# An MLP in four parts on one Trainium2 core: the second product of a part mixed with the first product of the next

## The chip, the cores and the metric

The kernel runs on one core of a Trainium2 chip. The metric is the device time of one execution in microseconds. The kernel before takes 1968.92 us (median of 3 runs, 1968.87 to 1968.93).

The core's engines work beside each other and meet through semaphores: TensorE (PE in the profile; PEld is its weight load) multiplies into PSUM, which has eight banks of 128 x 512 float32; VectorE (DVE) and ScalarE (ACT) work element by element and are the ones that empty PSUM here; GpSimd (POOL) works on SBUF; SyncE (SP) issues most of the loads.

## What is computed

A trunk of two layers over 256 tokens of width 2048, all in float32. Layer 0 mixes tokens by a convolution module, layer 1 by multi-head latent attention, and each is followed by the same kind of MLP, which holds the change:

```python
D_MODEL = 2048; SEQ = 256; DEPTH = 2; D_FF = 4 * D_MODEL

def sq_relu_mlp(h, w1, w2):
    return jnp.square(jax.nn.relu(h @ w1)) @ w2

for layer in range(DEPTH):
    h = rms_norm(x, norm_mixer_g[layer])
    x = x + mixer(h)            # convolution module or latent attention
    h = rms_norm(x, norm_mlp_g[layer])
    x = x + sq_relu_mlp(h, mlp_w1[layer], mlp_w2[layer])
return rms_norm(x, final_norm_g)
```

`w1` is 2048 x 8192 and `w2` 8192 x 2048, so a layer's MLP reads 128 MB of weights.

## The kernel before

**Three matmuls for one product.** Each float32 operand is split into a part `hi`, rounded to TensorE's float32r format by a copy on ScalarE (`split_into`, L412), and a part `lo = x - hi` on VectorE (L413). A product is hi·hi + lo·hi + hi·lo, three matmuls (`mm3`, L186 to L188). Weights come from HBM in raw units of 1 MB (`load`, L150, three buffers) and are split in chunks; six `hi` and six `lo` buffers (`WB = 6`) hold chunks that are ready.

**First product** (`up_unit`, L473). A group is 512 columns of `w1`. For each of 16 steps k along D and each of the group's four 128-column blocks there are two matmuls into the block's own bank: L488 multiplies `hi` of the weights by the activations' `hi` and `lo` side by side (512 columns: 256 tokens twice), and L489 `lo` of the weights by the activations' `hi` (256 columns). A group so fills four banks. `up_steps` then makes `g = relu(u)^2`: ScalarE copies one half of each bank out (L504), VectorE adds the other half (L506), then squares (L509 or L520), and the result is split as well. The RMS norm's factor is applied after the second product, as `r2` in L545.

**Second product** (`down_units`, L530). Two blocks of the hidden width make a *pair*. One pass covers two of the four 512-column blocks of the output, so with two token tiles a pair is a 2 x 2 by 2 x 2 block product. A *plain* pair (`plain_unit`) takes eight `mm3`, 24 matmuls. A pair in *Strassen's form* (`seven_unit`, in Winograd's variant) takes seven, 21 matmuls, into seven banks; for it GpSimd makes three sums of the activations (L513 to L517) when the pair's first product is done, and VectorE makes sums of the weights: L649 (two at once) and L662 (two) for each pair and pass, and these sums are split too. When a pass has done its last Strassen pair, `early` (L560) combines four of the seven banks (ScalarE copies L566 and L567, VectorE L568 and L569, GpSimd L574 and L575, VectorE L545); the other four results (three banks and one more, `Q0`) go on through the plain pairs, and `end` (L583) adds them to the residual `xs`.

**Order.** The hidden width is cut in `HALVES = 2`. Each half does its whole first product (8 groups) and then its second product in two passes (`n2`) over 16 pairs. `SEVENS` names which pairs of a half take Strassen's form: 7 of 16 in each half, in turn with plain ones. In the last pass of layer 1 the last three pairs are kept back and done by token tile, so that the final norm of one tile runs beside the other's matmuls (`finale`).

**Streaming.** `stream` (L415) runs over all units' chunks under a hand-written order (`manual_schedule`): before TensorE's work of a chunk it issues the split of the chunk five further on, and before each split one step of `todo` (the squares, the parts, `early`'s later steps). When a unit's last split is issued, the unit three further on is loaded. Each engine works its instructions off in this order.

Of the kernel before, what the change touches and what calls it, by code (L numbers as in the profile page):

```python
# [10 lines left out]
F32 = mybir.dt.float32  # L11
# [7 lines left out]
P = 128  # L19
# [7 lines left out]
W = 31  # L27
# [8 lines left out]
HALVES = 2  # L36
# [41 lines left out]
def trunk_kernel(  # L78
# [66 lines left out]
    def load(srcs, nj):  # L145

        raw = wpool.tile([P, nj, sum(src.shape[-1] for src in srcs)], F32, tag="raw", name=nm("raw"), bufs=3)
# [237 lines left out]
    NPAIR = FF // P // HALVES // 2  # L385
    N_SEVEN = len(SEVENS[0])
# [17 lines left out]
    class Chunk:  # L404
        def __init__(self, prep, run, after=(), now=None, flush=False):
            self.prep, self.run, self.after, self.now, self.flush = prep, run, after, now, flush
# [8 lines left out]
    def stream(units, todo):  # L415

        raws, parts, late = {}, {}, []

        def start(u):
            if u < len(units):  # L420
                raws[u] = load([units[u].src], units[u].nj)

        chunks = [(u, c) for u, unit in enumerate(units) for c in range(len(unit.chunks))]
        done = [0]

        def prep():
            n = done[0]
            if n == len(chunks):
                return
            done[0] += 1  # L430
            u, c = chunks[n]
            held = late[:]
            late.clear()
            if units[u].chunks[c].flush:
                while held:
                    held.pop(0)()
            more = units[u].chunks[c].prep(raws[u], parts.setdefault(u, {}))
# [4 lines left out]
            if c == units[u].last_read:  # L442
                start(u + 3)

        for u in range(3):
            start(u)
        for n, (u, c) in enumerate(chunks):
            while done[0] < min(n + WB, len(chunks)):
                prep()
                if todo:  # L450
                    todo.pop(0)()
            if done[0] == len(chunks):
                while late:
                    late.pop(0)()
                for fn in todo[: 2 if n < len(chunks) - 1 else None]:
                    todo.remove(fn)
                    fn()
            chunk = units[u].chunks[c]
            chunk.run(parts[u])
            if chunk.now is not None:  # L460
                chunk.now()
            todo += chunk.after
        while todo:
            todo.pop(0)()

    def mlp(layer, ssq, next_gain, finish=None, before=None, last_w1=None):

        w1, w2 = mlp_w1[layer], mlp_w2[layer]
        units, nkh = [], FF // P // HALVES
        r2 = small.tile([P, T], F32, tag="r2", name=nm("r2"))  # L470
        made_stage, pre = [], []

        def up_unit(hs, c0, u, ps, after):  # L473

            def chunk(h):
                def prep(raw, parts):
                    parts[h] = hi_lo(2)
                    split_into(parts[h], raw[:, 2 * h : 2 * h + 2, :])

                def run(parts):  # L480
                    if not ps:
                        ps.extend(acc_tile() for _ in range(4))
                    wh, wl = parts.pop(h)
                    for j in range(2):
                        k = 4 * u + 2 * h + j
                        for b in range(4):
                            bs = slice(b * P, (b + 1) * P)
                            nc.tensor.matmul(ps[b], wh[:, j, bs], xhl(k), start=k == 0, stop=False)  # L488
                            nc.tensor.matmul(ps[b][:, :S], wl[:, j, bs], xh(k), start=False, stop=k == KC - 1)  # L489

                return Chunk(prep, run, after if h == 1 else [])

            unit = Unit(rows(w1, 4 * u, 4, c0, NB), 4, [chunk(h) for h in range(2)])
            unit.last_read = 1
            return unit

        def up_steps(mp, hs, sevens, p, ps, b2):

            held = {}

            def square():
                v = mp.tile([P, 2, S], F32, tag="v", name=nm("v"), bufs=2)
                for b in range(2):
                    nc.scalar.activation(v[:, b, :], ps[2 * b2 + b][:, S:], AF.Copy)  # L504
                for b in range(2):
                    nc.vector.tensor_tensor(v[:, b, :], ps[2 * b2 + b][:, :S], v[:, b, :], op=ALU.add)  # L506
                if p in sevens:
                    f = mp.tile([P, 8, P], F32, tag="W", name=nm("W"), bufs=1)
                    nc.vector.scalar_tensor_tensor(  # L509
                        out=f[:, 0:4, :].rearrange("p (b t) n -> p b (t n)", b=2), in0=v, scalar=0.0, in1=v,  # L510
                        op0=ALU.max, op1=ALU.mult,
                    )
                    nc.gpsimd.tensor_tensor(  # L513
                        f[:, 4:6, :], f[:, 0:1, :].broadcast_to([P, 2, P]), f[:, 1:3, :], op=ALU.subtract
                    )
                    nc.gpsimd.tensor_tensor(f[:, 6, :], f[:, 1, :], f[:, 5, :], op=ALU.subtract)
                    nc.gpsimd.tensor_tensor(f[:, 7, :], f[:, 3, :], f[:, 6, :], op=ALU.subtract)  # L517
                    held["src"], shape, tag, n = f[:, 1:8, :], [P, 7, P], "s", N_SEVEN
                else:
                    nc.vector.scalar_tensor_tensor(out=v, in0=v, scalar=0.0, in1=v, op0=ALU.max, op1=ALU.mult)  # L520
                    held["src"], shape, tag, n = v, [P, 2, S], "g", NPAIR - N_SEVEN
# [6 lines left out]
            return square, part  # L528

        def down_units(mp, hs, sevens, hf, n2):  # L530

            last_seven = max(sevens)
            last = hf == HALVES - 1
# [21 lines left out]
            def plain(p, k, part, n, t):  # L555
                gh, gl = (a[:, k, t * P : (t + 1) * P] for a in hs[p])
                bs = n - na
                mm(outs[t, n], gh, gl, part[0][:, bs, :], part[1][:, bs, :], p == NPAIR - 1 and k == 1)

            def early():  # L560
                s1, s5 = (mp.tile([P, NB], F32, tag="v", name=nm("v"), bufs=2) for _ in range(2))
# [19 lines left out]
                return [first, second, third]  # L581
# [23 lines left out]
            def plain_unit(p):  # L605

                def chunk(k):
# [4 lines left out]
                    def run(parts):  # L612
                        if tail and p > last_seven:
                            if k == 0:
                                kept.append((p, parts))
                            if p == NPAIR - 1 and k == 1:
# [9 lines left out]
                    if k == 1 and p == NPAIR - 1 and not tail:  # L626
# [5 lines left out]
            def seven_unit(p):  # L632
# [31 lines left out]
                def t24(raw, parts):  # L664
# [4 lines left out]
                    Chunk(one, run([("P1", A11, "one", 0)]), flush=True),  # L669
# [14 lines left out]
            for p in range(NPAIR):  # L684
                chunks, last_read = seven_unit(p) if p in sevens else plain_unit(p)
                unit = Unit(rows(w2, hf * nkh + 2 * p, 2, na * NB, 2 * NB), 2, chunks)
# [4 lines left out]
        with ExitStack() as cx:  # L691
            mp = cx.enter_context(tc.tile_pool(name=f"mp{layer}", bufs=1, reuse_waits="tile"))
            todo = []
# [5 lines left out]
            for hf in range(HALVES):  # L699
                hs, sevens = {}, SEVENS[2 * layer + hf]  # L700
                for g in range(nkh // 4):
                    ps = []
                    for u in range(KC // 4):
                        after = []
                        if u == KC // 4 - 1:
                            (sa, pa), (sb, pb) = (up_steps(mp, hs, sevens, 2 * g + b2, ps, b2) for b2 in range(2))
                            after = [sa, sb, pa, pb]
                            if g == nkh // 4 - 1 and hf == 0:
                                after.append(norm)
                            if g == nkh // 4 - 1 and hf == HALVES - 1 and last_w1 is not None:  # L710
                                after.append(last_w1)
                        units.append(up_unit(hs, (hf * nkh + 4 * g) * P, u, ps, after))
                for n2 in range(NNB // 2):
                    units += down_units(mp, hs, sevens, hf, n2)

            with tc.manual_schedule():
                stream(units, todo)
# [985 lines left out]
```

## Time and profile before

| | |
|---|---|
| median of 3 runs | 1968.92 us |
| the profiled execution | 1969.05 us, its span 1966.9 us |
| TensorE busy | 1939.8 us (99%), 10892 matmuls |
| VectorE busy | 1521.8 us (77%) |
| ScalarE busy | 1070.4 us (54%) |
| GpSimd busy | 334.8 us (17%) |
| read from HBM | 363.68 MB, 186 GB/s with what is written, over the span |
| layer 0's MLP begins | 318.6 us (first L488) |
| layer 1's MLP | 1270.2 us to the end |

The span is the time from the first to the last instruction; the execution's own time is 2.15 us more. Busy times of TensorE count overlapping matmuls once, so they say nothing on how dense the matmuls are; for that one divides a stretch by the number of matmuls in it. The columns of a group of instructions are: line, engine, operation, tile written <- tiles read, shapes, count | busy us, mean ns of one | idle time of the engine just before them, and what ended it. In a timeline a row is the start, the duration, the engine, the line and the instruction.

### The profile page before, as it was taken

What the parts mean: (1) busy time and instruction counts of PE and PEld (TensorE: products, weight loads), DVE (VectorE), ACT (ScalarE), POOL (GpSimd) and SP (SyncE); (2) the same over time, 40 slices, a digit from 0 to 9 for tenths busy, and PEclk for the clock granted to TensorE, in tenths of its full rate; (3) what the DMA queues carried; (4) which work ended last, traced back from release to release, by engine and by line L of the source; (5) the groups of instructions that cost most, each with busy time, mean ns of one, the idle gap of its engine ahead of it and who ended that gap; (6) DMA issues with size and microseconds to landing.
All of it is one profiled execution on the core that took longest, in us unless ns stands there. A gap on an engine that the chain in (4) does not pass through costs nothing.

```text
span 1966.9 us, 28422 instructions
## 1 busy us (share of the span) xinstructions
PE 1939.8 (99%) x10892; PEld 1695.0 (86%) x10892; DVE 1521.8 (77%) x2123; ACT 1070.4 (54%) x1511; POOL 334.8 (17%) x284
## 2 busy tenths in 40 slices
PE   7999999999999999999999999999999999999998
PEld 7999888888888888888899998888888888888886
DVE  5999866666899777689886665566689986668897
ACT  5556655454555545455576665544456554455555
POOL 5999300111000011100001410011100001110000
PEclk9999999999999999999999999999999999999999
DMA  8666455656566765656656445566657676665663
GB/s 237 178 186 179 142 188 185 187 179 191 176 208 201 227 188 183 192 187 195 213 167 182 118 147 180 184 186 191 188 164 229 193 222 190 193 193 189 219 191 130
DMA packets 210503, 367.61 MB, mean 187 GB/s; under 512 B 15416, under 2 KB 89792, under 8 KB 210112
## 3 DMA queue, kind: packets, MB, share of 16 engines
q1 hardware_dynamic: 209344, 363.63, 59.6%
q10 hardware_dynamic: 1024, 2.17, 0.3%
q8 instruction: 85, 1.39, 0.3%
q14 instruction: 50, 0.41, 0.1%
HBM read 363.68 MB, written 2.10 MB: 186 GB/s over the span
## 4 chain that ended last, share of the span: by engine, by line
PE 94%; DVE 2%; ACT 1%; DMA 1%; issue 1%; POOL 0%; POOLq 0%; DVEq 0%; ACTq 0%; SPq 0%
PE acc L488 24%; PE acc L186 15%; PE acc L187 15%; PE acc L188 15%; PE acc L489 12%; PE acc L775 3%; PE acc L774 3%; PE acc L773 3%; PE acc L242 1%; PE sum L823 0%; DVE lo L413 0%; PE acc L1471 0%; DMA xs<-in_x 0%; DMA raw<-in_mlp_w 0%; PE acc L1335 0%
## 5 line engine op out<-in xcount | busy, mean ns | idle before, releaser
L413 DVE TENSOR_TENSOR lo<-raw,hi 128x1024 fp32r<-128x1024 f32 (+1 forms) x512 | 610.6, 1203 | 282.0 <-ACT hi L412 279.6
L412 ACT ACTIVATE hi<-raw 128x1024 fp32r<-128x1024 f32 (+1 forms) x512 | 512.9, 1012 | 480.4 <-PE acc L488 317.4
L488 PE MATMUL acc<-xt,hi 128*128 128x512 f32 x2048 | 713.8, 393 | 0.0
L489 PE MATMUL acc<-xt,lo 128*128 128x256 f32 x2048 | 574.4, 280 | 0.0
L488 PEld LDWEIGHTS acc<-xt,hi 128*128 128x128 f32 x2048 | 384.4, 188 | 88.1
L489 PEld LDWEIGHTS acc<-xt,lo 128*128 128x128 f32 x2048 | 385.3, 188 | 0.1
L186 PE MATMUL acc<-hi,gh 128*128 128x512 f32 x576 | 224.3, 389 | 0.0
L188 PE MATMUL acc<-lo,gh 128*128 128x512 f32 x576 | 224.1, 389 | 0.0
L187 PE MATMUL acc<-hi,gl 128*128 128x512 f32 x576 | 224.1, 389 | 0.0
L412 ACT ACTIVATE hi<-T 128x1024 fp32r<-128x1024 f32 x112 | 119.1, 1064 | 159.8 <-DVE T L662 103.6
L186 PE MATMUL acc<-hi,sh 128*128 128x512 f32 x520 | 203.5, 391 | 1.5 <-DVE v L506 1.5
L160 ACT ACTIVATE hi<-raw 128x1024 fp32r<-128x1024 f32 (+2 forms) x184 | 179.9, 1005 | 42.2 <-PE acc L187 38.2
L188 PE MATMUL acc<-lo,sh 128*128 128x512 f32 x520 | 202.8, 390 | 0.0
L161 DVE TENSOR_TENSOR lo<-raw,hi 128x1024 fp32r<-128x1024 f32 (+2 forms) x118 | 133.2, 1147 | 65.1 <-ACT hi L160 59.5
L875 DVE SCALAR_TENSOR_TENSOR sum<-ub,w_dw,sum 128x256 f32<-128x256 f32 x400 | 162.7, 478 | 7.6 <-ACT sum L831 6.5
L161 POOL TENSOR_TENSOR lo<-raw,hi 128x1024 fp32r<-128x1024 f32 x66 | 157.5, 2410 | 24.2 <-ACT hi L160 24.2
L513 POOL TENSOR_TENSOR W<-W 128x256 f32<-128x256 f32 x28 | 21.8, 779 | 800.3 <-ACT hi L412 622.1
L187 PE MATMUL acc<-hi,sl 128*128 128x512 f32 x392 | 152.5, 389 | 0.0
L413 DVE TENSOR_TENSOR lo<-T,hi 128x1024 fp32r<-128x1024 f32 x112 | 136.8, 1221 | 11.1 <-ACT hi L412 8.4
L773 PE MATMUL acc<-xt,hi 128*128 128x256 f32 x512 | 145.3, 284 | 0.0
L774 PE MATMUL acc<-xt,hi 128*128 128x256 f32 x512 | 143.9, 281 | 1.0 <-DVE xt L199 1.0
L775 PE MATMUL acc<-xt,lo 128*128 128x256 f32 x512 | 144.0, 281 | 0.0
(262 smaller groups left out, 2864.9 us busy)
## 6 DMA issues: line engine op xcount, KB each, us to landing
raw<-in_mlp_w SPq DMA_DIRECT2D x256, 1024.0 KB, 5.6
raw<-in_conv_w_pw SPq DMA_DIRECT2D x64, 512.0 KB, 5.5
raw<-in_conv_w_pw SPq DMA_DIRECT2D x16, 1024.0 KB, 5.2
raw<-in_mla_w_o SPq DMA_DIRECT2D x16, 1024.0 KB, 5.9
raw<-in_mla_w_kv_up SPq DMA_DIRECT2D x8, 1024.0 KB, 5.5
raw<-in_mla_w_in SPq DMA_DIRECT2D x8, 576.0 KB, 3.9
raw<-in_mla_w_in SPq DMA_DIRECT2D x4, 1024.0 KB, 6.8
raw<-in_mla_w_q_up SPq DMA_DIRECT2D x16, 256.0 KB, 3.8
```

Source lines behind the costliest of these rows:

```text
L160: nc.scalar.activation(hi, raw[:, js, :], AF.Copy)
L161: eng.tensor_tensor(lo, raw[:, js, :], hi.bitcast(F32), op=ALU.subtract)
L186: nc.tensor.matmul(ps, sh, mh, start=start, stop=False)
L187: nc.tensor.matmul(ps, sl, mh, start=False, stop=False)
L188: nc.tensor.matmul(ps, sh, ml, start=False, stop=stop)
L412: nc.scalar.activation(parts[0], src, AF.Copy)
L413: nc.vector.tensor_tensor(parts[1], src, parts[0].bitcast(F32), op=ALU.subtract)
L488: nc.tensor.matmul(ps[b], wh[:, j, bs], xhl(k), start=k == 0, stop=False)
L489: nc.tensor.matmul(ps[b][:, :S], wl[:, j, bs], xh(k), start=False, stop=k == KC - 1)
L773: nc.tensor.matmul(o, wh[:, bs], xh(k), start=k == 0, stop=False)
L774: nc.tensor.matmul(o, wh[:, bs], xl(k), start=False, stop=False)
L775: nc.tensor.matmul(o, wl[:, bs], xh(k), start=False, stop=k == KC - 1)
```

## The change

- **Four parts.** `PARTS = 4` in place of two halves: a part has 8 pairs. A pass over the output is made for each part, so there are 8 passes in a layer instead of 4, each with its `early` and `end`.
- **Mixing.** The first product of part 0 runs alone. Then, while a part's second product runs, the first product of the next part is mixed in: `MIX = (2, 1, 1, 2, 1, 1, 2)` says how many halves of Strassen pairs (a half is two of the four chunks) follow each first-product block; an eighth block follows the first plain pair. The last part has nothing to mix in.
- **One bank.** A first-product unit is now one 128-column block over all 16 steps (its load reads rows of 512 bytes, before 2 KB), into one bank. ScalarE copies the whole bank into a tile `U` right after the block's last matmul; sum and square then read SBUF.
- **More Strassen pairs.** `SEVENS` names 5 of 8 pairs in the first three parts and 3 (layer 0) or 2 (layer 1) of 8 in the last.
- **Smaller things.** A fourth raw buffer (`pool`); a block before a single half has the splits issued one chunk less ahead (`LOOK_UP = 5`, `tight`); the step of `todo` is issued ahead of the split, not after it; `early`'s two subtractions move from GpSimd to VectorE.

```diff
-HALVES = 2
+PARTS = 4
+LOOK_UP = 5
-SEVENS = ((1, 3, 5, 7, 9, 11, 13),) * 3 + ((0, 2, 4, 6, 8, 10, 12),)
+MIX = (2, 1, 1, 2, 1, 1, 2)
+N_S, N_G = 7, 6
+SEVENS = tuple(((3, 4, 5, 6, 7),) * 3 + (last,) for last in ((0, 2, 4), (0, 2)))
+MADE = tuple((range(8),) * 3 + (last,) for last in ((0, 1, 2, 3, 5, 4, 6, 7), range(8)))
+LATE_G = ((6, 7), (5, 6, 7))
...
-        for u in range(3):
-            start(u)
-        for n, (u, c) in enumerate(chunks):
-            while done[0] < min(n + WB, len(chunks)):
-                prep()
-                if todo:
-                    todo.pop(0)()
+        for home in (None, None, None, pool):
+            start(home)
+        for n, (unit, c) in enumerate(chunks):
+            chunk = unit.chunks[c]
+            while done[0] < min(n + (LOOK_UP if chunk.tight else WB), len(chunks)):
+                if todo:
+                    todo.pop(0)()
+                prep()
...
+            def up_unit(b):
+                ps = []
+
+                def chunk(h):
+                    def prep(raw, parts):
+                        parts[h] = [a.rearrange("p a (j n) -> p (a j) n", n=P) for a in hi_lo(2)]
+                        split_into(parts[h], raw[:, 8 * h : 8 * h + 8, :])
+
+                    def run(parts):
+                        if not ps:
+                            ps.append(acc_tile())
+                        wh, wl = parts.pop(h)
+                        for j in range(8):
+                            k = 8 * h + j
+                            nc.tensor.matmul(ps[0], wh[:, j, :], xhl(k), start=k == 0, stop=False)
+                            nc.tensor.matmul(ps[0][:, :S], wl[:, j, :], xh(k), start=False, stop=k == KC - 1)
+
+                    def out():
+                        if b == 0:
+                            held["u"] = u_tile()
+                        nc.scalar.activation(held["u"][:, b, :], ps[0], AF.Copy)
+
+                    if h == 0:
+                        return Chunk(prep, run)
+                    return Chunk(prep, run, [square, lambda: None, part] + extra if b == 1 else [], now=out)
+
+                unit = Unit(rows(w1, 0, KC, ((q * NPAIR + p) * 2 + b) * P, P), KC, [chunk(h) for h in range(2)])
...
             def square():
-                v = mp.tile([P, 2, S], F32, tag="v", name=nm("v"), bufs=2)
-                for b in range(2):
-                    nc.scalar.activation(v[:, b, :], ps[2 * b2 + b][:, S:], AF.Copy)
-                for b in range(2):
-                    nc.vector.tensor_tensor(v[:, b, :], ps[2 * b2 + b][:, :S], v[:, b, :], op=ALU.add)
+                v = held["u"][:, :, :S]
+                nc.vector.tensor_tensor(v, v, held["u"][:, :, S:], op=ALU.add)
...
                 def second():
                     xs_add(nb, s1, 1)
                     xs_add(nb, v, 0)
-                    nc.gpsimd.tensor_tensor(u, s5, u, op=ALU.subtract)
-                    nc.gpsimd.tensor_tensor(v, s5, v, op=ALU.subtract)
 
                 def third():
+                    nc.vector.tensor_tensor(u, s5, u, op=ALU.subtract)
+                    nc.vector.tensor_tensor(v, s5, v, op=ALU.subtract)
+
+                def fourth():
                     xs_add(na, u, 1)
                     xs_add(na, v, 0)
...
+            hs = {}
+            for unit in ups(hs, 0):
+                put(unit)
+            for q in range(PARTS):
+                now, hs = hs, {}
+                more = ups(hs, q + 1) if q < PARTS - 1 else []
                 for n2 in range(NNB // 2):
-                    units += down_units(mp, hs, sevens, hf, n2)
+                    units = down_units(mp, now, q, n2)
+                    if not more:
+                        for unit in units:
+                            put(unit)
+                        continue
+                    halves = [(units[p], cs) for p in SEVENS[layer][q] for cs in ((0, 1), (2, 3))]
+                    for n in MIX:
+                        put(more.pop(0))
+                        chunks[-1][0].chunks[1].tight = n == 1
+                        for unit, cs in halves[:n]:
+                            put(unit, cs)
+                        del halves[:n]
+                    for i, p in enumerate(p for p in range(NPAIR) if p not in SEVENS[layer][q]):
+                        if i == 1:
+                            put(more.pop(0))
+                        put(units[p])
```

More of the change, by code (lines that the diff above doesn't have):

```diff
@@ L143, in tr_tile, with load @@
         return psum["tr"].tile([P, NB], F32, tag="tr", name=nm("tr")) if "tr" in psum else acc_tile()
-    def load(srcs, nj):
-        raw = wpool.tile([P, nj, sum(src.shape[-1] for src in srcs)], F32, tag="raw", name=nm("raw"), bufs=3)
+    def load(srcs, nj, pool=None):
+        shape = [P, nj, sum(src.shape[-1] for src in srcs)]
+        if pool is None:
+            raw = wpool.tile(shape, F32, tag="raw", name=nm("raw"), bufs=3)
+        else:
+            raw = pool.tile(shape, F32, tag="more", name=nm("raw"), bufs=1)
         at = 0
@@ L404, in trunk_kernel, with __init__ @@
     class Chunk:
-        def __init__(self, prep, run, after=(), now=None, flush=False):
-            self.prep, self.run, self.after, self.now, self.flush = prep, run, after, now, flush
+        def __init__(self, prep, run, after=(), now=None):
+            self.prep, self.run, self.after, self.now, self.tight = prep, run, after, now, False
     def hi_lo(n):
@@ L413, in split_into, with stream, start @@
         nc.vector.tensor_tensor(parts[1], src, parts[0].bitcast(F32), op=ALU.subtract)
[L415 to L423, printed above, removed]
+    def stream(chunks, todo, pool):
+        units = list(dict.fromkeys(unit for unit, _ in chunks))
+        raws, parts, late, homes = {}, {}, [], {}
+        def start(home):
+            if len(raws) < len(units):
+                unit = units[len(raws)]
+                homes[unit] = home
+                raws[unit] = load([unit.src], unit.nj, home)
         done = [0]
@@ L430, in prep @@
             done[0] += 1
-            u, c = chunks[n]
+            unit, c = chunks[n]
             held = late[:]
             late.clear()
[L434 to L437, printed above, removed]
+            more = unit.chunks[c].prep(raws[unit], parts.setdefault(unit, {}))
             if more is not None:
@@ L457, in stream @@
                     fn()
-            chunk = units[u].chunks[c]
-            chunk.run(parts[u])
+            chunk.run(parts[unit])
             if chunk.now is not None:
@@ L468, in mlp @@
         w1, w2 = mlp_w1[layer], mlp_w2[layer]
-        units, nkh = [], FF // P // HALVES
         r2 = small.tile([P, T], F32, tag="r2", name=nm("r2"))
[L471 to L495, printed above, removed]
@@ L507, in square @@
                 if p in sevens:
-                    f = mp.tile([P, 8, P], F32, tag="W", name=nm("W"), bufs=1)
+                    f = f_tile()
                     nc.vector.scalar_tensor_tensor(
@@ L526, in part, with down_units @@
                 split_into(hs[p], held["src"])
-            return square, part
-        def down_units(mp, hs, sevens, hf, n2):
+            return [up_unit(b) for b in range(2)]
+        def down_units(mp, hs, q, n2):
+            sevens = SEVENS[layer][q]
             last_seven = max(sevens)
-            last = hf == HALVES - 1
+            last_plain = max(p for p in range(NPAIR) if p not in sevens)
+            last = q == PARTS - 1
             if last and not made_stage:
@@ L557, in plain @@
                 bs = n - na
-                mm(outs[t, n], gh, gl, part[0][:, bs, :], part[1][:, bs, :], p == NPAIR - 1 and k == 1)
+                mm(outs[t, n], gh, gl, part[0][:, bs, :], part[1][:, bs, :], p == last_plain and k == 1)
             def early():
-                s1, s5 = (mp.tile([P, NB], F32, tag="v", name=nm("v"), bufs=2) for _ in range(2))
+                while todo:
+                    todo.pop(0)()
+                s1, s5 = (a[:, i, :] for a in [u_tile()] for i in range(2))
                 uv = mp.tile([P, 2, NB], F32, tag="W", name=nm("W"), bufs=1)
@@ L625, in chunk @@
                         after = [next_prepare]
[L626 removed]
+                    if k == 1 and p == last_plain and not tail:
                         return Chunk(prep, run, now=end)
@@ L685, in down_units @@
                 chunks, last_read = seven_unit(p) if p in sevens else plain_unit(p)
-                unit = Unit(rows(w2, hf * nkh + 2 * p, 2, na * NB, 2 * NB), 2, chunks)
+                unit = Unit(rows(w2, 2 * (q * NPAIR + p), 2, na * NB, 2 * NB), 2, chunks)
                 unit.last_read = last_read
@@ L697, in norm, with put @@
                 nc.vector.tensor_tensor(r2, r, r, op=ALU.mult)
[L699 to L712, printed above, removed]
-                for n2 in range(NNB // 2):
-                    units += down_units(mp, hs, sevens, hf, n2)
+            def put(unit, cs=None):
+                chunks.extend((unit, c) for c in (range(len(unit.chunks)) if cs is None else cs))
@@ new lines, in ups @@
+            def ups(hs, q):
+                end = norm if q == 0 else last_w1 if q == PARTS - 1 else None
+                return [
+                    unit for p in MADE[layer][q]
+                    for unit in up_units(hs, q, p, [end] if p == MADE[layer][q][-1] and end is not None else [])
+                ]
+            hs = {}
[4 more added lines that the diff above has]
+                more = ups(hs, q + 1) if q < PARTS - 1 else []
+                for n2 in range(NNB // 2):
+                    units = down_units(mp, now, q, n2)
[14 more added lines that the diff above has]
+                        put(units[p])
```

35 lines of the change are left out of this document (22 added, 13 removed).

## The prediction

> **What bounds the kernel now.** I read the head of the page first, then its chain of waits, then the engines by stretches of the MLP.
>
> ```profile
> span 1966.9 us, 28422 instructions
> PE 1939.8 (99%) x10892; PEld 1695.0 (86%) x10892; DVE 1521.8 (77%) x2123; ACT 1070.4 (54%) x1511; POOL 334.8 (17%) x284
> PE 94%; DVE 2%; ACT 1%; DMA 1%; issue 1%; POOL 0%; POOLq 0%; DVEq 0%; ACTq 0%; SPq 0%
> ```
>
> TensorE is busy for 99% of the span and is 94% of the chain that ends last. The next view gives three stretches: the convolution, a second product (505 to 660) and a first product (670 to 840).
>
> ```profile
> core 0: us, PE busy (x) PEld busy (x) DVE busy (x) ACT busy (x) POOL busy (x), PEclk, DMA share, GB/s
> 60.00:195.00 135.00, 135.00 (x1144) 135.00 (x1144) 133.80 (x345) 74.76 (x124) 128.21 (x83) 1.00 0.67 183
> 505.00:660.00 155.00, 155.00 (x685) 128.38 (x685) 143.45 (x155) 90.26 (x97) 6.60 (x4) 1.00 0.65 207
> 670.00:840.00 170.00, 170.00 (x983) 149.42 (x982) 112.41 (x119) 82.55 (x104) 20.00 (x21) 1.00 0.62 192
> ```
>
> In both MLP stretches TensorE has no idle time, at the full granted clock. What differs is VectorE: busy 143.45 of 155 us (93%) in the second product, 112.41 of 170 us (66%) in the first. So the kernel ends earlier only by fewer or denser matmuls, and the reserve from which a change could spend is VectorE's: 7% in one phase, 34% in the other.
>
> As busy matmuls overlap, I price one by the pitch: 155/685 = 0.2263 us for 512 columns, and 170/983 = 0.173 us on average in the first product, 0.346 us for a pair of 512 and 256 columns. The timeline agrees:
>
> ```profile
> 503.02 0.39 PE L186 MATMUL acc<-hi,gh 128*128 128x512 f32 x1
> 503.25 0.39 PE L187 MATMUL acc<-hi,gl 128*128 128x512 f32 x1
> 1274.08 0.39 PE L488 MATMUL acc<-xt,hi 128*128 128x512 f32 x1
> 1274.31 0.28 PE L489 MATMUL acc<-xt,lo 128*128 128x256 f32 x1
> 1274.43 0.39 PE L488 MATMUL acc<-xt,hi 128*128 128x512 f32 x1
> ```
>
> **The change, part by part. Matmuls removed.** A plain pair costs 8 triples (24 matmuls) in each of the two passes over the output columns, a pair in Strassen's form 7 (21).
>
> ```profile
> L186 PE MATMUL acc<-hi,gh 128*128 128x512 f32 x576 | 224.3, 389 | 0.0
> L187 PE MATMUL acc<-hi,sl 128*128 128x512 f32 x392 | 152.5, 389 | 0.0
> ```
>
> 392 = 7 x 28 pairs x 2 passes, 576 = 8 x 36 x 2. The new tables name 5+5+5+3 pairs in layer 0 and 5+5+5+2 in layer 1, 35 of 64 (not 40: the last part has fewer). Seven more pairs x 2 passes x 3 matmuls = 42 matmuls x 0.2263 = **9.5 us**, all on the path. The first product keeps its 2048 pairs of matmuls.
>
> **A stall removed.** The MLP's one visible wait of TensorE stands where the last second product begins and its banks are still being emptied by the first product's four-bank group:
>
> ```profile
> 1796.62 0.47 PE L186 MATMUL acc<-hi,sh 128*128 128x512 f32 x1 [1.50 <-DVE v L506]
> ```
>
> With the first products a part ahead and one bank each, no four banks are emptied there: **1.5 us** saved.
>
> **One bank for the first product.** All 32 matmuls of a block now follow each other in one bank; before, every pair changed banks. The nearest row is the convolution, whose three 256-column matmuls share a bank:
>
> ```profile
> 100.00 0.28 PE L773 MATMUL acc<-xt,hi 128*128 128x256 f32 x1
> 100.12 0.28 PE L774 MATMUL acc<-xt,hi 128*128 128x256 f32 x1
> 100.24 0.28 PE L775 MATMUL acc<-xt,lo 128*128 128x256 f32 x1
> ```
>
> 0.12 us within a bank, and 0.12 from L489 to L488 across banks: I take zero. The rows resolve 0.01 us at best, hence bounds of some 0.002 us either way on 2048 joints, -4 to +4 us.
>
> **VectorE in an interleaved half-part.** This decides the rest. A half-part (one pass of one part, 12 in all) is 8 first-product blocks, 5 Strassen pairs, 3 plain pairs. TensorE: 8 x 16 x 0.346 + 5 x 21 x 0.2263 + 3 x 24 x 0.2263 = 84.3 us. VectorE's prices, from the second product (510 to 655):
>
> ```profile
> L413 DVE TENSOR_TENSOR lo<-raw,hi 128x1024 fp32r<-128x1024 f32 x46 | 55.7, 1219 | 9.3 <-ACT hi L412 9.3
> L413 DVE TENSOR_TENSOR lo<-T,hi 128x1024 fp32r<-128x1024 f32 x26 | 31.8, 1222 | 0.6
> L662 DVE TENSOR_TENSOR T<-T,raw 128x512 f32<-128x512 f32 x26 | 18.0, 692 | 0.9
> L649 DVE TENSOR_TENSOR T<-raw 128x1024 f32<-128x1024 f32 x12 | 14.6, 1217 | 0.0
> L413 DVE TENSOR_TENSOR lo<-raw,hi 128x512 fp32r<-128x512 f32 x13 | 10.0, 768 | 0.0
> L545 DVE SCALAR_TENSOR_TENSOR xs<-acc,r,xs 128x512 f32<-128x512 f32 x4 | 2.7, 742 | 0.0
> L568 DVE TENSOR_TENSOR W<-v,acc 128x512 f32<-128x512 f32 x2 | 1.4, 679 | 0.0
> L413 DVE TENSOR_TENSOR gl<-v,gh 128x512 fp32r<-128x512 f32 x1 | 0.7, 683 | 0.0
> ```
> ```profile
> 548.81 1.22 DVE L649 TENSOR_TENSOR T<-raw 128x1024 f32<-128x1024 f32 x1
> 549.94 1.82 DVE L413 TENSOR_TENSOR lo<-raw,hi 128x512 fp32r<-128x512 f32 x2
> ```
>
> A 1.22 us instruction is followed by an independent one after 1.13, so I take 0.08 off those that depend on nothing just before them. A Strassen pair: 1.14 + 0.69 + 1.14 + 1.22 + 2 x 0.69 + 1.22 = 6.8 us. Every other unit is two splits, 2.28 us. Emptying the seven banks: 8 x 0.66 + 2 x 0.68 + the two subtractions that move from GpSimd to VectorE, 2 x 0.69, = 8.0 us. A finished pair of the first product: sum 0.69, squared relu 0.69, split 1.09 (Strassen) or 0.68 (plain), the sums from these rows:
>
> ```profile
> L413 DVE TENSOR_TENSOR lo<-raw,hi 128x1024 fp32r<-128x1024 f32 x54 | 69.9, 1294 | 50.2 <-ACT hi L412 50.2
> L413 DVE TENSOR_TENSOR sl<-W,sh 128x896 fp32r<-128x896 f32 x7 | 7.6, 1085 | 0.0
> L413 DVE TENSOR_TENSOR gl<-v,gh 128x512 fp32r<-128x512 f32 x7 | 6.6, 947 | 0.0
> L520 DVE SCALAR_TENSOR_TENSOR v<-v 128x512 f32<-128x512 f32 x7 | 4.8, 691 | 0.2
> ```
>
> The heavier half-part is the second, with four Strassen pairs to finish (by MADE order the first has one): 11 x 2.28 + 5 x 6.8 + 8.0 + 4 x 2.47 = 77 us of 84.3, 91%, the share at which the second product of before runs with TensorE never idle. Its splits are ready five to six chunks early; the shortest such run of chunks (the four of a Strassen pair and one of the first product) lasts 4.8 + 2.8 = 7.5 us. The worst local surplus, a block and a whole Strassen pair (TensorE 5.5 + 4.8, VectorE 2.3 + 6.8 + 2.5 for a finished pair), is 1.3 us: hidden.
>
> **GpSimd between.** The last rows were taken at 340 to 495, while GpSimd makes each Strassen pair's sums:
>
> ```profile
> L516 POOL TENSOR_TENSOR W<-W 128x128 f32<-128x128 f32 x7 | 9.3, 1323 | 0.6
> L517 POOL TENSOR_TENSOR W<-W 128x128 f32<-128x128 f32 x7 | 5.5, 792 | 0.6
> L513 POOL TENSOR_TENSOR W<-W 128x256 f32<-128x256 f32 x7 | 5.2, 736 | 249.1 <-ACT hi L412 131.5 <-DVE W L509 117.6
> ```
>
> There the split takes 1294 instead of 1219 ns and the plain pair's 947 instead of 683: (54 x 75 + 7 x 264) ns = 5.9 us over 7 pairs, 0.84 us a pair with VectorE 66% busy, by proportion 1.2 us at 91%. Bounds: 0, and all of GpSimd's time, 1.32 + 0.79 + 0.74 = 2.85 us. I take 1.2: 4 x 1.2 + 77 = 82 us, still under 84.3, nothing on the path. The Trainium skill ("SBUF — State Buffer", Who interferes with whom) states more: a VectorE instruction with two SBUF inputs and a GpSimd one that reads SBUF exclude each other for the whole instruction. By that rule alone the price is the upper bound and the sum would be rival 1's; the trace's 0.84 is under a third of it.
>
> **Emptying one bank.** The copy out of the block's bank is a new kind of step on ScalarE (the nearest row, 512 columns, is below). Behind it wait the next block's first matmul and ScalarE's further splits. Its cover is the work before the next block: at least half a Strassen pair, 9 x 0.2263 = 2.04 us.
>
> ```profile
> L412 ACT ACTIVATE hi<-raw 128x1024 fp32r<-128x1024 f32 x46 | 48.5, 1059 | 21.4 <-PE acc L187 17.5 <-DVE xs L545 1.4 <-DMA raw<-in_mlp_w 0.9
> L566 ACT ACTIVATE v<-acc 128x512 f32<-128x512 f32 x2 | 1.2, 578 | 0.0
> ```
>
> 0.58, even behind a whole split 1.06 + 0.58 = 1.64 us: hidden.
>
> **Weights in 512-byte rows.** The first product's loads get the convolution's row length.
>
> ```profile
> raw<-in_mlp_w SPq DMA_DIRECT2D x256, 1024.0 KB, 5.6
> ```
>
> There 183 GB/s take 0.67 of the queues; a half-part moves 16 such loads, 16.8 MB in 84.3 us, 199 GB/s, at that rate 0.73. SP's loads are a fourth tile ahead, so nothing new waits: zero.
>
> **New waits of TensorE.** The last part has no blocks to mix in: per pass VectorE has 3 x 6.8 + 5 x 2.28 + 8.0 = 39.8 us of TensorE's 41.6 in layer 0 (96%), 35.3 of 42.2 in layer 1. So it can be behind when a pass ends, and a Strassen pair's fifth bank comes 12 x 0.2263 = 2.7 us after the pass before, and is free after 0.74 us unless VectorE is behind by more than two splits. Four such places, 0 to 1.1 us each: I allow 1 us in all, bounds 0 and 4.4. At the layer's start the first block now needs all of xt within some 4 us, where before it needed a quarter:
>
> ```profile
> 1271.65 0.39 PE L488 MATMUL acc<-xt,hi 128*128 128x512 f32 x1
> 1272.28 1.66 DVE L199 SCALAR_TENSOR_TENSOR xt<-acc,vecs,xt 128x256 fp32r<-128x256 f32 x4 [0.24 <-ACT xt L192]
> ```
>
> The last quarter is ready at 1273.94; ten steps of 0.346 from 1271.65 put its use at 1275.1: hidden by 1.2 us.
>
> **Sum.** 1966.9 - 9.5 - 1.5 + 1.0 = 1956.9 us of span. The profiled execution took 1969.05, 2.15 more than its span, and the median is 0.13 below that: 1956.9 + 2.15 - 0.13 = **1958.9 us**. A measurement of this kernel can tell some 0.2%, 3.9 us, from no change.
>
> **Rivals.** *1, VectorE becomes the bound (slower).* Each Strassen pair's sums on GpSimd block VectorE for their full 2.85 us. The second half-part then needs 77 + 4 x 2.85 = 88.4 us against 84.3; 4.1 x 6 second half-parts = 25 us, 1984. It decides from (84.3 - 77)/4 = 1.8 us a pair. For it: the splits and the T sums all read two SBUF tiles. Against: the measured 0.84. Chance 0.09, a third of it near no change.
> *2, the block's bank comes back late.* Two splits ahead of the copy make 2 x 1.06 + 0.58 = 2.70 us against 2.04, 0.66 us in the 24 places where only the shorter half of a Strassen pair lies between: 16 us, 1975; at half of them 1967, no change. Against: one split fewer is issued ahead exactly there, and ScalarE is 58% busy. Chance 0.07, somewhat more than half of it slower.
> *3, the pitch in one bank is off.* 0.005 us more per joint is 10 us, 1969. Chance 0.04, mostly near no change.
>
> **How the numbers follow.** The forecast has 0.80. Its own range: the new waits' bounds give 1957.9 to 1962.3, the pitch's bounds about half their width more, 1956 to 1964. With part of the cases near no change the range is 1956 to 1967. Faster 0.80; within 0.2% 0.08; slower 0.12.
>
> **What would show it.** L187 on sl 490 times, L186 on gh 464. Right: in the interleaved stretches TensorE without idle time, VectorE at 91 to 97%. Wrong, rival 1: waits of TensorE for lo in second passes, and T<-T or lo above 1.3 us; rival 2: first matmuls of a block waiting for ScalarE's copy; rival 3: L488 to L488 off 0.346. If TensorE waits more than 11 us in the MLP, the forecast of a gain is wrong.

## The result and the profile after

The changed kernel takes 1973.38 us (median of 14 runs, 1971.65 to 1975.15), the kernel before on the same chips 1968.89 us (14 runs, 1965.27 to 1969.04). The ratio is 1.0025, 95% interval 1.0017 to 1.0033: slower, where 1958.9 us was forecast. (Both kernels' runs fall on a few values some microseconds apart; the last section says where these steps are seen.)

The head of the page after:

```profile
span 1971.2 us, 28450 instructions
PE 1937.5 (98%) x10850; PEld 1685.6 (86%) x10850; DVE 1623.1 (82%) x2241; ACT 1108.2 (56%) x1555; POOL 348.9 (18%) x289
PE 85%; DVE 6%; POOL 3%; ACT 3%; issue 2%; DMA 0%; SPq 0%; POOLq 0%; DVEq 0%; ACTq 0%
```

TensorE has the 42 matmuls fewer (10892 to 10850), and the chain that ends last has gone from 94% TensorE to 85%; GpSimd, at 0% of it before, has 3%. The groups of instructions say who is waited for:

```profile
L197 PE MATMUL acc<-lo,sh 128*128 128x512 f32 x698 | 274.2, 393 | 6.3 <-DVE lo L421 6.3
L195 PE MATMUL acc<-hi,sh 128*128 128x512 f32 x698 | 274.9, 394 | 3.1 <-ACT hi L420 3.1
L529 POOL TENSOR_TENSOR W<-W 128x256 f32<-128x256 f32 x35 | 55.6, 1588 | 1136.9 <-DVE W L525 1009.6
```

TensorE waits for weights' splits, `lo` from VectorE and `hi` from ScalarE, and GpSimd's first sum takes 1588 ns, where its mean over the span was 779 before (736 in the stretch that the prediction shows). Where in a part this happens is seen by stretches; these are the first and the second pass of layer 0's first mixed part:

```profile
core 0: us, PE busy (x) PEld busy (x) DVE busy (x) ACT busy (x) POOL busy (x), PEclk, DMA share, GB/s
409.00:495.00 86.00, 86.00 (x441) 73.22 (x440) 76.75 (x90) 50.67 (x61) 7.12 (x6) 1.00 0.66 196
495.00:580.00 85.00, 83.33 (x424) 70.02 (x423) 74.78 (x78) 45.82 (x55) 14.29 (x12) 1.00 0.65 193
```

The first pass has no idle TensorE, the second has, though VectorE is busy there for 88% only; in the kernel before's second product it was busy for 93% and TensorE waited nowhere. So VectorE is not full; it comes late because it waits itself. The chain of waits over one such place, in order of time (start, duration, what):

```profile
510.61 0.13 PE acc L505
...
510.77 0.61 ACT U L510
...
511.40 0.70 DVE U L522
...
512.12 0.70 DVE W L525
...
512.96 1.60 POOL W L529
...
514.63 0.80 POOL W L532
...
515.50 0.80 POOL W L533
...
516.33 0.96 ACT sh L420
...
518.32 0.93 DVE lo L421
519.24 0.21 issue
519.45 1.23 DVE lo L421
520.68 0.04 issue
520.73 0.50 PE acc L197
```

A block that completes a Strassen pair ends at 510.74. ScalarE copies it out, VectorE sums and squares, GpSimd makes its three sums until 516.30, ScalarE splits the pair (`sh`), and only then the weights' splits follow. TensorE comes to the matmul that needs the last of them at 520.05 (519.82 and one pitch of 0.23) and can start it at 520.73:

```profile
519.82 0.39 PE L196 MATMUL acc<-hi,sl 128*128 128x512 f32 x1
520.73 0.50 PE L197 MATMUL acc<-lo,sh 128*128 128x512 f32 x1 [0.52 <-DVE lo L421]
521.06 0.40 PE L195 MATMUL acc<-hi,sh 128*128 128x512 f32 x1
```

With the slower start behind it (0.33 to the next matmul) the place costs 0.8 us. The pair itself is needed a part later; nothing on this chain is urgent but its last link. The view of ScalarE there shows why the last link hangs on the others:

```profile
510.77 0.60 ACT L510 ACTIVATE U<-acc 128x512 f32<-128x512 f32 x1 [4.72 <-PE acc L505]
511.26 1.05 ACT L420 ACTIVATE hi<-T 128x1024 fp32r<-128x1024 f32 x1
516.33 0.95 ACT L420 ACTIVATE sh<-W 128x896 fp32r<-128x896 f32 x1 [4.01 <-POOL W L533]
517.18 1.04 ACT L420 ACTIVATE hi<-raw 128x1024 fp32r<-128x1024 f32 x1
518.13 1.05 ACT L420 ACTIVATE hi<-T 128x1024 fp32r<-128x1024 f32 x1
```

ScalarE stands for 4.0 us at `sh`, with the weights' splits behind it, and VectorE, whose half of the pair's split is queued ahead of the next `lo`, stands for 1.3 us for `sh`. That makes theory A: the split of the finished pair (`part`) is issued so early that ScalarE waits in order for GpSimd. Theory B is rival 1 of the prediction in its plain form: VectorE has too much work in the second pass. Theory C is rival 2: the copy out of the one bank is in the way.

### The profile page after: what moved, and what is told of

It reads as the page before. It is cut to its first block, busy times and chain, and to the rows that moved or that the text cites. A ratio compares the mean times of both kernels' runs of the same rounds, so it can differ in the third digit from the quotient of the medians.

```text
span 1971.2 us, 28450 instructions
## 1 busy us (share of the span) xinstructions
PE 1937.5 (98%) x10850; PEld 1685.6 (86%) x10850; DVE 1623.1 (82%) x2241; ACT 1108.2 (56%) x1555; POOL 348.9 (18%) x289
## 4 chain that ended last, share of the span: by engine, by line
PE 85%; DVE 6%; POOL 3%; ACT 3%; issue 2%; DMA 0%; SPq 0%; POOLq 0%; DVEq 0%; ACTq 0%
PE acc L504 20%; PE acc L197 14%; PE acc L195 14%; PE acc L196 14%; PE acc L505 10%; DVE lo L421 3%; PE acc L816 3%; PE acc L815 3%; PE acc L814 3%; POOL W L529 1%; DVE T L685 1%; ACT hi L420 1%; ACT sh L420 1%; POOL W L533 1%; POOL W L532 1%
## 5 line engine op out<-in xcount | busy, mean ns | idle before, releaser
L505 PE MATMUL acc<-xt,lo 128*128 128x256 f32 x2048 | 574.1, 280 | 0.0
L197 PE MATMUL acc<-lo,sh 128*128 128x512 f32 x698 | 274.2, 393 | 6.3 <-DVE lo L421 6.3
L195 PE MATMUL acc<-hi,sh 128*128 128x512 f32 x698 | 274.9, 394 | 3.1 <-ACT hi L420 3.1
L529 POOL TENSOR_TENSOR W<-W 128x256 f32<-128x256 f32 x35 | 55.6, 1588 | 1136.9 <-DVE W L525 1009.6
L196 PE MATMUL acc<-hi,sl 128*128 128x512 f32 x570 | 222.3, 390 | 0.0
L510 ACT ACTIVATE U<-acc 128x512 f32<-128x512 f32 x128 | 76.0, 594 | 202.6 <-PE acc L505 202.6
L197 PEld LDWEIGHTS acc<-lo,sh 128*128 128x128 f32 x698 | 131.1, 188 | 40.0 <-DVE lo L421 11.5
L195 PEld LDWEIGHTS acc<-hi,sh 128*128 128x128 f32 x698 | 131.0, 188 | 32.8 <-ACT hi L420 5.6
L195 PE MATMUL acc<-hi,gh 128*128 128x512 f32 x384 | 149.6, 390 | 0.0
L197 PE MATMUL acc<-lo,gh 128*128 128x512 f32 x384 | 149.5, 389 | 0.0
L196 PE MATMUL acc<-hi,gl 128*128 128x512 f32 x384 | 149.4, 389 | 0.0
```

The lines of the kernel that those rows point to most:

```text
L195: nc.tensor.matmul(ps, sh, mh, start=start, stop=False)
L196: nc.tensor.matmul(ps, sl, mh, start=False, stop=False)
L197: nc.tensor.matmul(ps, sh, ml, start=False, stop=stop)
L505: nc.tensor.matmul(ps[0][:, :S], wl[:, j, :], xh(k), start=False, stop=k == KC - 1)
L510: nc.scalar.activation(held["u"][:, b, :], ps[0], AF.Copy)
L529: nc.gpsimd.tensor_tensor(f[:, 4:6, :], f[:, 0:1, :].broadcast_to([P, 2, P]), f[:, 1:3, :], op=ALU.subtract)
```

## The experiments

Each ratio is to the kernel before on the same chip; the changed kernel's is 1.0025.

| run | ratio (95% interval) | span, us | ScalarE's wait for GpSimd's sums, us | TensorE idle for `hi` or `lo` in the MLP |
|---|---|---|---|---|
| the changed kernel | 1.0025 (1.0017 to 1.0033) | 1971.2 | 103.0 | yes |
| e1_late_part | 0.9946 (0.9932 to 0.9959) | 1956.0 | none seen | no |
| e2_dve_sums | 0.9949 (0.9933 to 0.9965) | 1960.0 | 32.4, for VectorE's sums | 0.2 us at one place in a mixed part |
| e3_four_of_eight | 1.0057 (1.0043 to 1.0071) | 1979.0 | 76.7 | yes |
| e4_order | 0.9960 (0.9946 to 0.9974) | 1958.1 | 96.4 | four places in all |
| e5_look6 | 0.9954 (0.9936 to 0.9972) | 1954.4 | 95.9 | no |
| e6_one_step | 0.9951 (0.9936 to 0.9966) | 1956.6 | 32.4 | no |
| e7_four_late | 0.9990 (0.9981 to 1.0000) | 1964.7 | none seen | no |
| e8_late_more | 0.9950 (0.9932 to 0.9967) | 1957.7 | none seen | one place, last part |

In comparing spans one thing has to be kept apart: the two first products that run unmixed, one in each layer, have one of two pitches (last section), and the slower one costs some 1.7 us for each. By the traces none of the two has it in e4 and e5, one in the changed kernel, e1, e3, e6 and e7, both in e2 and e8.

**The split of the pair issued later.**

```diff
-return Chunk(prep, run, [square, lambda: None, part] + extra if b == 1 else [], now=out)
+return Chunk(prep, run, [square] + [lambda: None] * (1 if q == 0 else 4) + [part] + extra if b == 1 else [], now=out)
```

> The changed kernel with one edit: in the mixed parts the split of a finished pair of the first product (the step part) is issued three steps of todo later, so that ScalarE's copy in it no longer stands waiting for GpSimd's three sums. Theory A (GpSimd's sums take 3.7 us here, ScalarE waits for them in order, the weights' splits queued behind it come late and TensorE waits): nearly all of the 14 us of TensorE's visible waits go, 1961 us give or take 2. Theory B (VectorE simply has too much work in the second pass of a part): nothing moves, 1973 us. Theory C (the copy out of the one bank blocks ScalarE): nothing moves, 1973 us.

Measured 1959.93 us, 0.9946: what had been forecast for the change itself (0.9949). The span is 15.2 us below the changed kernel's, with the same matmuls on TensorE and one first product at the slower pitch in both. Its ScalarE at the same place:

```profile
509.36 1.05 ACT L420 ACTIVATE hi<-T 128x1024 fp32r<-128x1024 f32 x1
510.30 1.05 ACT L420 ACTIVATE hi<-raw 128x1024 fp32r<-128x1024 f32 x1
514.18 1.06 ACT L420 ACTIVATE hi<-T 128x1024 fp32r<-128x1024 f32 x1 [2.82 <-DVE T L685]
...
517.50 0.94 ACT L420 ACTIVATE sh<-W 128x896 fp32r<-128x896 f32 x1
```

The weights' splits that stood behind `sh` (`hi<-raw` at 510.30, `hi<-T` at 514.18) now go ahead of it, and `sh` starts without a wait for GpSimd, whose sums run from 511.05 to 514.38 here. The second pass is full, and VectorE does more in it than in the changed kernel:

```profile
495.00:580.00 85.00, 85.00 (x436) 72.37 (x435) 79.52 (x83) 48.29 (x56) 14.30 (x12) 1.00 0.67 199
```

With 79.52 of 85 us (94%) VectorE keeps up. Theory B falls here, and C with it: both had said that nothing moves.

**GpSimd's sums on VectorE.**

```diff
-nc.gpsimd.tensor_tensor(f[:, 4:6, :], ...)
-nc.gpsimd.tensor_tensor(f[:, 6, :], ...)
-nc.gpsimd.tensor_tensor(f[:, 7, :], ...)
+nc.vector.tensor_tensor(f[:, 4:6, :], ...)
+nc.vector.tensor_tensor(f[:, 6, :], ...)
+nc.vector.tensor_tensor(f[:, 7, :], ...)
```

> The changed kernel with GpSimd's three sums of a Strassen pair's activations made on VectorE instead, some 1 us a pair there. Theory A: the sums are ready 2 to 3 us earlier and nothing blocks VectorE's shared reads, so most waits go: 1963 us give or take 3. Theory B: VectorE gets 4 us more in each of the heavier passes that are already too full, 6 such passes: slower, 1985 us or more. Theory C: 1973 us.

Measured 1960.89 us, 0.9949. VectorE takes more work and the kernel gets faster, the opposite of B. The sums on VectorE:

```profile
L529 DVE TENSOR_TENSOR W<-W 128x256 f32<-128x256 f32 x6 | 2.5, 425 | 0.2
L533 DVE TENSOR_TENSOR W<-W 128x128 f32<-128x128 f32 x6 | 1.8, 293 | 0.2
L532 DVE TENSOR_TENSOR W<-W 128x128 f32<-128x128 f32 x6 | 1.8, 292 | 0.2
```

1.0 us of work in place of 3.6 us of GpSimd's time, so the chain is that much shorter; small waits stay (two of about 0.1 us at one place in a mixed part).

**Four Strassen pairs of eight.**

```diff
-MIX = (2, 1, 1, 2, 1, 1, 2)
-SEVENS = tuple(((3, 4, 5, 6, 7),) * 3 + (last,) for last in ((0, 2, 4), (0, 2)))
+MIX = (2, 1, 1, 1, 1, 1, 1)
+SEVENS = tuple(((4, 5, 6, 7),) * 3 + (last,) for last in ((0, 2, 4), (0, 2)))
```

The order in which pairs are made (`MADE`) and the buffers of the split pairs (`N_S`, `N_G` and which pair uses which) are changed to match.

> The changed kernel with 4 instead of 5 Strassen pairs of 8 in the mixed parts (single halves between all blocks but the first two, and the order in which pairs are made adapted to the buffers). TensorE has 6 pairs x 6 matmuls x 0.227 = 8.2 us more work. Theory A: pairs with GpSimd sums still finish in front of single halves, so about two thirds of the 14 us of waits stay: 1977 us. Theory B: VectorE's load per pass falls by 6.8 - 2.3 = 4.5 us and the waits go: 1973.4 + 8.2 - 14.2 = 1967 us. Theory C: more single halves, more waits: 1980 us or more.

Measured 1980.75 us, 1.0057, 3.8 us above what A said. VectorE is relieved (71.48 of 87 us, 82%, in the second pass of layer 0's first mixed part) and the waits stay:

```profile
495.00:582.00 87.00, 85.52 (x432) 71.65 (x431) 71.48 (x75) 45.45 (x54) 9.51 (x9) 1.00 0.66 194
```

So B is out again. That A's figure was low is explained by the places: with single halves nearly everywhere, three in this pass wait (519.67, 536.52, 553.35, each for `lo` from VectorE); over the span it is 16 waits to the changed kernel's 18, while A had counted on two thirds of them. By itself this run did not tell A from C, which had expected 1980 or more; e7 does.

**Another order of the pairs.**

```diff
-MADE = tuple((range(8),) * 3 + (last,) for last in ((0, 1, 2, 3, 5, 4, 6, 7), range(8)))
+MADE = tuple((range(8),) + ((0, 3, 1, 4, 5, 6, 2, 7),) * 2 + (last,) for last in ((1, 0, 3, 2, 5, 4, 6, 7), (1, 0, 3, 2, 4, 5, 6, 7)))
```

> The changed kernel with the same work, but the next part's pairs are made in another order: the Strassen ones finish at the blocks that are followed by a whole Strassen pair or by plain pairs, all but one a part. Theory A: waits stay only at the one remaining place in two of three mixed parts, 0.8 us x 4 of 14 us: 1962 us give or take 2. Theory B: the work of VectorE in a part is the same but spread evenly over both passes; if the heavier pass was too full, part of the waits goes, 1968 us. Theory C: nothing moves, 1973 us.

Measured 1961.76 us, 0.9960, as A said. ScalarE's wait is hardly shorter (96.4 us), but a single half needs a split right behind it less often. The work on each engine is the same, and in layer 0's first mixed part a single wait is left, after the one Strassen pair that still finishes before a single half:

```profile
519.12 0.50 PE L197 MATMUL acc<-lo,sh 128*128 128x512 f32 x1 [0.53 <-DVE lo L421]
```

**One chunk more ahead.**

```diff
-LOOK_UP = 5
+LOOK_UP = 6
```

> The changed kernel with LOOK_UP = 6: in front of a single half the split of one more chunk is issued ahead, as everywhere else. It stands before the copy out of the bank in ScalarE's queue, and part is popped one split later. Theory A (ScalarE's in-order wait for GpSimd's sums): part comes some 1 to 2 us later and one chunk more is ready, so the waits shrink or go, 1960 to 1966 us. Theory C (the copy out of the one bank is late): the copy stands behind one split more, the waits grow, 1975 us or more, and first matmuls of a block wait for ScalarE's copy.

Measured 1959.19 us, 0.9954. Theory C is refuted: the copy out of the bank stands behind one split more, and no block waits for it. A is narrowed: ScalarE's wait is nearly as long as in the changed kernel. The waits for `sh` of the changed kernel and of this one, over the whole span:

```profile
ACT sh L420 <- POOL W L533: 103.0, 25, 4.7
```
```profile
ACT sh L420 <- POOL W L533: 95.9, 25, 4.7
```

But one more chunk is ready when it begins, and that covers it. So the wait costs time only together with the shorter lookahead that the change sets in front of single halves.

**One step later.**

```diff
-return Chunk(prep, run, [square, lambda: None, part] + extra if b == 1 else [], now=out)
+return Chunk(prep, run, [square] + [lambda: None] * (1 if q == 0 else 2) + [part] + extra if b == 1 else [], now=out)
```

> The changed kernel with part issued one step of todo later in the mixed parts (e1_late_part moved it by three). Theory A: one weights' split passes ahead of the wait on GpSimd; that is one chunk of 1.4 to 2.8 us more in hand where TensorE waited 0.7 to 1.6 us in all at a place, so most waits go and some of 0.1 to 0.5 us may stay: 1960 to 1965 us. Theory C: no change from the changed kernel, 0.25% above the kernel before.

Measured 1958.74 us, 0.9951, no waits of TensorE for `hi` or `lo` left; ScalarE's wait is down to 32.4 us. One step later is enough.

**Four of eight, and the later split.** The edits of e3_four_of_eight and e1_late_part together.

> e3_four_of_eight (4 Strassen pairs of 8 in the mixed parts) with part three steps later as in e1_late_part. Theory A, and the price of a matmul by its pitch: no waits, and 36 matmuls x 0.2267 = 8.2 us more than e1_late_part's 0.9946 of the kernel before, so 0.9988 of it. Theory C (more single halves, so the bank's copy is in the way more often): waits of about 12 us stay, 1.005.

Measured 0.9990 of the kernel before, as A said (0.9988). The waits of e3 were A's, not C's. Against e6_one_step the span is 8.1 us longer (1964.7 to 1956.6) for 36 matmuls more, 0.225 us each: the pitch that the prediction used holds as a price (layer 0's first product has the slower pitch in both).

**A third Strassen pair in layer 1's last part.**

```diff
-SEVENS = tuple(((3, 4, 5, 6, 7),) * 3 + (last,) for last in ((0, 2, 4), (0, 2)))
+SEVENS = tuple(((3, 4, 5, 6, 7),) * 3 + (last,) for last in ((0, 2, 4), (0, 2, 4)))
```

This stands on top of e1_late_part's edit, with `MADE` to match.

> e1_late_part with a third Strassen pair in layer 1's last part (3 of 8, as in layer 0). Theory A: 6 matmuls fewer, 1.4 us less than e1_late_part if VectorE, which then has some 96% of that part's time as in layer 0's, still keeps up: 0.994 of the kernel before. If VectorE is the bound there (theory B's place, the last part), it gives back 1 us or more: no better than e1_late_part.

Measured 0.9950 (0.9932 to 0.9967), no better than e1_late_part. In that part a wait has come:

```profile
1935.90 0.50 PE L197 MATMUL acc<-lo,sh 128*128 128x512 f32 x1 [0.82 <-DVE lo L421]
```

The matmul before it starts at 1934.70, so 1.20 - 0.23 = 1.0 us of the 1.4 us saved goes back: here, with no block to mix in, VectorE is late.

So four small edits make the change the gain it was forecast to be; the best ratios, 0.9946 (e1), 0.9949 (e2), 0.9951 (e6) and 0.9954 (e5), cannot be told apart, though at an equal pitch e2's span is some 2 us longer than the others'.

## Why the prediction was wrong

- **The step that failed** is the wait: "VectorE in an interleaved half-part" put the waits of the mixed parts at nothing ("hidden", "nothing on the path"), and "New waits of TensorE" looked for them only in the last parts and at a layer's start. Behind both stands the costing of `part`. The prediction listed a finished pair's split only as VectorE's time (1.09 or 0.68 us) and GpSimd's sums only as time in which VectorE may be blocked. It did not count `part` as an instruction on ScalarE that waits in order for GpSimd, nor name the weights' splits queued behind it. The row was there to be read; over the whole span of the kernel before the waits view says:

```profile
ACT sh L412 <- POOL W L517: 3.8, 15, 0.5
```

  0.5 us at most. There a group finished two pairs at once and one pair's steps lay between the other's; now the pairs finish singly, the three sums take 3.6 us in place of 2.85, and 3.8 us became 103.0. At the place shown the steps from the block's end to the last `lo` take 9.9 us, and TensorE had 9.3 us of work; the prediction had held its cover of five to six chunks against a surplus of 1.3 us of VectorE alone. It had also counted the shorter lookahead before single halves as help against rival 2 and not asked what it takes from that cover (e5: one chunk more, and no wait). Such waits come 18 times, at some 0.8 us, 14 us in all, more than the 11 us that the prediction named as the sign of being wrong. The price was 15.2 us of span (the changed kernel against e1), against nothing allowed for the mixed parts; the 1 us that was allowed, 4.4 at most, was for the last parts, where no wait came.
- **Rival 1** had the sign, GpSimd's part and mostly the place right, and the mechanism wrong. Four of the six mixed parts wait in the second pass; the third of each layer waits in the first (layer 0's at 780 and 817 to 819 us), where by the order of making most Strassen pairs of the last part finish. The rival asked when VectorE has more work than time. VectorE's work was about right (82 of 84.3 us forecast, 79.52 of 85 in e1) and TensorE waits for it in no mixed part of e1; what made it late was a delay in another queue.
- **GpSimd beside VectorE.** VectorE's loss was below the 1.2 us taken: the weights' double sum takes 1380 ns beside GpSimd and 1219 in e2 without it, the half split 817 and 685, the single sums 720 and 692. That is (10 x 161 + 10 x 132 + 20 x 28) ns over six pairs, 0.6 us a pair. The other side was not priced: GpSimd's first sum went from 736 to some 1590 ns. The Trainium skill ("SBUF — State Buffer", Who interferes with whom) has the later of the two instructions wait for the earlier one's end, where a VectorE instruction has two SBUF inputs and the GpSimd one reads SBUF. The trace agrees so far as instructions of both engines take longer beside each other, by the figures above; on which engine the loss falls is what the prediction did not ask.
- **Matmuls removed**: right, 42 fewer, and the price confirmed (0.225 us by e7 against e6). The expected count of names was off: L196 on `sl` runs 570 times and L195 on `gh` 384, not 490 and 464, since five late plain pairs, in two passes each, keep their split in the `s` buffers (80 triples); the sum, 954, is as forecast.
- **The stall removed**: right; no wait stands at the start of the last part.
- **One bank**: right, the pitch of a pair is 0.346 us as before. What was missed are the joints between blocks and Strassen halves, below.
- **The copy out of the bank** and **the loads in 512-byte rows**: right. No first matmul of a block waits (e5 with a split more in front), and no wait of TensorE in the MLP is put down to a DMA.
- **The last part**: no wait in the changed kernel where 96% was forecast (layer 0); TensorE's times there, 183 and 186 matmuls a pass, come to 41.4 and 42.1 us at 0.2263, not 41.6 and 42.2, which changes nothing. e8 shows how near that is to the edge.
- **The sum, by spans.** -9.5 (matmuls) - 1.5 (old stall) + 15.2 (against e1) makes +4.2; 1971.2 - 1966.9 is +4.3. The joints (+3.3, below) are in it too. Against them stand 1.7 us, since only half as much first product runs at the slower pitch, and 1.5 us that no run takes apart. So it is partly luck that e1, where only these small terms are left, comes so near the forecast (a span of 1956.0 against 1956.9).

## What to carry to other kernels

When work moves next to other work, write down for each step which queue it is issued on, what it waits for there and what stands behind it, and not only how long it keeps its engine busy: a step that nobody needs soon can hold up one that is needed at once. An engine that is waited for and is itself not full (VectorE at 88% here, where it reached 94% in e1 without making TensorE wait) is a hint that the cause lies further up; follow the chain of waits back past it before removing work from it. Here the cheapest cure was to issue the step that isn't urgent later.

## What the runs showed of the hardware

- **Joints cost a little.** After a block of the first product the first matmuls of a Strassen half come slower. This half of nine, in the changed kernel, starts at 425.76, and the next block at 427.83 (next row): 2.07 us, where nine at 0.2267 take 2.04.

```profile
425.76 0.40 PE L195 MATMUL acc<-hi,sh 128*128 128x512 f32 x1
...
427.83 0.40 PE L504 MATMUL acc<-xt,hi 128*128 128x512 f32 x1
```

  The 24 such halves of nine in that trace, none of which holds a wait, take 2.075 us on average, so a joint costs some 0.035 us, and the 96 joints of the mixed parts 3.3 us. Why was not tried.
- **Two pitches of the first product.** In the kernel before, a long first product runs at one of two pitches. The rows of layer 0's first half and of layer 1's:

```profile
340.00:495.00 155.00, 155.00 (x880) 134.58 (x879) 103.81 (x112) 75.35 (x98) 19.95 (x21) 1.00 0.61 188
1280.00:1445.00 165.00, 165.00 (x955) 145.01 (x954) 110.30 (x117) 80.57 (x102) 20.22 (x21) 1.00 0.62 191
```

  0.3523 and 0.3456 us a pair of matmuls, at the same clock; 512 pairs of the slower make 3.4 us, and the times of the kernel before lie 3.5 us apart (1965.3, 1968.9, 1972.3). In the changed kernel and its variants the unmixed first product is half as long, and their times lie 1.7 us apart (1971.7, 1973.4, 1975.1). Which of the two an execution gets differs between executions of one kernel; what decides it stays open.
- **These three sums are slow on GpSimd and cost VectorE time from there too.** They take 1.0 us on VectorE (e2), and 3.6 us on GpSimd plus 0.6 us that VectorE loses. In the chain above that makes 2.6 us; on VectorE's time alone GpSimd still saves 0.4 us a pair.
